# Hybrid encoder layer, attention sweep: GpSimd's half of the softmax sums no longer ordered behind VectorE's, residual additions and four output pieces moved, GpSimd's work placed beside maxima in the short sequence

## The chip, the cores and the metric

One Trainium2 chip, one core of it. The metric is the device time of one execution in microseconds (us). TensorE (PE) does matmuls, its weight loads are PEld; VectorE is DVE, ScalarE is ACT, GpSimd is POOL, SyncE (SP) issues the DMAs. Each engine takes its own instructions strictly in the order in which the program lists them; across engines they wait on semaphores.

## The reference, cut to what matters

One encoder layer runs on two sequences with shared weights: a "prompt" of 1024 tokens (the short one, `s == 0`) and a "sample" of 2048 tokens (`s == 1`), both of width 1024.

```python
h = rms_norm(x, norm_pre)
u_pool, g_pool, q, k, v, g_attn, q_x, g_x = split(h @ w_in)
pool_out = multiscale_pool(u_pool) * silu(g_pool)                     # 256 columns
attn_out = softmax(q k^T / 8) v * silu(g_attn)                        # 8 heads, 2 key heads, 512 columns
x_out    = softmax(q_x k_m^T / 8) v_m * silu(g_x)                     # 4 heads, 256 memory tokens, 256 columns
y = concat(pool_out, attn_out, x_out) @ w_out
return x + rms_norm(y, norm_post)
```

The change is in the softmax sums, the gating, the output product `y` and the last line.

## The kernel before, in words

The first stage (to about 708 us) projects both sequences and puts q, k, v and the gates into DRAM scratch. The second stage is the attention sweep, and the change is all in it. It works through 12 pairs (a pair is 256 query tokens): the sample's eight first (pairs 0 to 7), then the prompt's four (8 to 11). A pair has three groups: key head 0, the memory attention, key head 1 (the first pair has the memory group first). A group with key head 0 or 1 has 16 chunks of 128 keys in the sample and 8 in the prompt; a memory group has 2. A turn does two chunks, so a sample pair takes 17 turns. The order of all instructions on all engines is written out by hand: a loop over turns, and a table `later` of steps that are due at a turn or a fraction of one (`at(turn + 1.1, f, ...)` puts f there, `due` emits it).

In one turn:

- `weights`: PE makes the scores S of a chunk (L231), ACT takes the exponential into P (L233, 128x1024: two heads' halves of 512). P has five buffers.
- `sums`: z, the running sum of the P of a group, is added up elementwise. In the sample `CUT` is 512: DVE adds the upper 512 columns (L244), POOL the lower 512 (L246). In the prompt `CUT` is 0, and DVE adds all 1024 (L244). The odd chunk of a turn is added early in the next turn (`before.sums(kb + 1)`), the even one in the turn itself.
- `largest` looks ahead for a later group: PE scores into the single PSUM buffer N (L189, L181), and DVE takes the maxima of it (L197, L199 after a copy by ACT in L196, or L201). The next N can't start until these have read the last one.
- `values` (L260) multiplies P with V; at a group's end `totals` (L269) has PE sum z over partitions. So totals needs the last L244 and the last L246 of the group.
- `project` adds output pieces (L393 to L395, three matmuls a piece; 8 pieces make one half of an output row block, 32 a pair) in the turns without `values`. When a half is done ACT squares it (L399) and DVE scales it (L411); when both are, POOL makes the norm's factor (L415, L418), ACT scales y (L427), POOL adds the residual into xr (L428), SP stores it (L436).
- `store_mix` is the gating: POOL multiplies a group's result with its gate and 1/z (L304; `pu` is the pooling mixer's tile), ACT casts the high part (L307), POOL subtracts for the low part (L311). Both parts feed the output pieces. In the last pair DVE does this work in POOL's place.

The lines that a sentence can't say:

```python
v = nc.vector.tensor_tensor(out=z[:, cut:], in0=a[:, cut:], in1=P[:, cut:], op=ALU.add)        # L244
e = nc.gpsimd.tensor_tensor(out=z[:, :cut], in0=a[:, :cut], in1=P[:, :cut], op=ALU.add)        # L246
if k < self.chunks - 1:
    behind(e, v)          # POOL's half starts only when DVE's half has ended; not in a group's last chunk
...
HOLD, PIECES = (13, 21), (8, 4)                                                                # L446
for _ in range(PIECES[turns[turn][0].s] if turn < len(turns) else 8):                          # L979
```

Of the kernel before, what the change touches and what calls it, by code (L numbers as in the profile page):

```python
# [23 lines left out]
def encoder(ctx, tc, I, O):  # L24
# [28 lines left out]
    mhalf = const.tile([128, 8], F32, name="mhalf")  # L53
    nc.vector.memset(mhalf, -0.5)

    def behind(later, first):
        tc.add_manual_dep(later.ins, first.ins.name,
                          mybir.DependencyInfo(mybir.DependencyClass.Sync, mybir.DependencyReason.DATA),
                          reason="one after the other")

    def rsqrt(pool, ss, n, count, tag):

# [71 lines left out]
    class Group:  # L134
# [100 lines left out]
        def sums(self, k):  # L235
            if k == 0:
                return
            if k == 1:
                self.z = dbl.tile([128, 2, 512], F32, name="z", tag="z")
            flat = "p j q -> p (j q)"  # L240
            z, P = self.z.rearrange(flat), self.P[k].rearrange(flat)
            a = self.P[0].rearrange(flat) if k == 1 else z
            cut = CUT[self.s]
            v = nc.vector.tensor_tensor(out=z[:, cut:], in0=a[:, cut:], in1=P[:, cut:], op=ALU.add)  # L244
            if cut:
                e = nc.gpsimd.tensor_tensor(out=z[:, :cut], in0=a[:, :cut], in1=P[:, :cut], op=ALU.add)  # L246
                if k < self.chunks - 1:
                    behind(e, v)

        def values(self, ks):  # L250

# [48 lines left out]
    def store_mix(slot, pair, c, a, b, v="p (c t q) -> p c t q"):  # L300

        a, b = a.rearrange(v, c=2, t=2), b.rearrange(v, c=2, t=2)
        e = nc.vector if pair.last else nc.gpsimd
        e.tensor_tensor(out=a, in0=a, in1=b, op=ALU.mult)  # L304

        def high():
            nc.scalar.copy(out=pair.parts()[0][:, c:c + 2], in_=a)  # L307

        def low():
            hi, lo = [m[:, c:c + 2] for m in pair.parts()]  # L310
            e.tensor_tensor(out=lo, in0=a, in1=hi.bitcast(F32), op=ALU.subtract)  # L311

        after = (0, 0, pair.s, pair.s)[c // 2]
        begin = max(slot, pair.free + after)
        soon = pair.s == 0 and not pair.last and c < 4
        at(begin + (0.6 if soon else 1.4), high)
        at(begin + (0.6 if soon else 1.6), low)
# [42 lines left out]
    class Output:  # L360
# [41 lines left out]
        def scale(self, h):  # L402
            if h == 0 and not self.last:
                for m in sorted(later):
                    for x in [x for x in later[m] if x[0].__name__ in ("norm", "out", "store")]:
                        later[m].remove(x)
                        f, args = x
                        f(*((args[0], None) if f.__name__ == "out" else args))
                self.start()
            c = slice(512 * h, 512 * h + 512)  # L410
            nc.vector.tensor_tensor(out=self.y[:, c], in0=self.ps[h], in1=npost[:, c], op=ALU.mult)  # L411
# [8 lines left out]
        def out(self, h, after):  # L420
            x, y = self.xr, self.y
            c = slice(512 * h, 512 * h + 512)
            if self.last:
                nc.vector.scalar_tensor_tensor(out=x[:, c], in0=y[:, c], scalar=self.r[:, 0:1], in1=x[:, c],  # L424
                                               op0=ALU.mult, op1=ALU.add)
            else:
                nc.scalar.activation(out=y[:, c], in_=y[:, c], func=AF.Copy, scale=self.r[:, 0:1])  # L427
                nc.gpsimd.tensor_tensor(out=x[:, c], in0=x[:, c], in1=y[:, c], op=ALU.add)  # L428
            if after is None:
                self.store(h)  # L430
            else:
                at(after, self.store, h)
# [25 lines left out]
    def at(turn, f, *args):  # L458

        later.setdefault(round(turn, 2), []).append((f, args))  # L460
# [8 lines left out]
    fill = []  # L469
# [505 lines left out]
    def project(turn):  # L975

        if turn in value_runs or not fill:
            return
        for _ in range(PIECES[turns[turn][0].s] if turn < len(turns) else 8):  # L979
            out, h, c, start, final = fill.pop(0)  # L980
            out.piece(h, c, start, final, turn >= looked)
            if final:
                out.square(h)
                end = out.last or turn >= len(turns)
                if end:
                    out.scale(h)
                else:
                    at(turn + 1.1, out.scale, h)
                if h == 1:
                    slow = not end and turns[turn][0].s == 1  # L990
                    at(turn + (0.6 if end else 1.6 if slow else 1.4), out.norm)
                    for x in range(2):
                        if out.last:
                            at(turn + 0.6, out.out, x, None)
                        else:
                            z = turn + (2.4 + x if slow else 1.6)
                            at(z, out.out, x, None if end else z + 0.8)
                break

    with tc.manual_schedule(engines=order):  # L1000
        turn = 0
        while turn < len(turns) or later or fill:
# [67 lines left out]
```

## Time and profile before

| what | value |
|---|---|
| time, median of 3 runs | 1760.3 us (1760.29 to 1761.58) |
| the profiled execution: its time, its span | 1756.41 us, 1754.5 us |
| PE busy, share of the span | 1686.4 us, 96% |
| DVE, ACT, POOL busy | 1122.1, 792.3, 830.9 us |
| sample part of the sweep, with the first pair | 708 to about 1440 us |
| prompt part of the sweep | about 1440 to 1754 us |
| L244 (DVE's sums), L246 (POOL's sums), z<-z,P groups | 268.1 us in 272; 299.3 us in 224 |

Busy time is the union of an engine's instructions; idle before a group is the time in which its engine did nothing just before it, and behind the arrow stands what ended that idle time. PEclk is the clock that PE was granted, as a share of full speed.

### The profile page before, as it was taken

How to read it: one execution, taken by the hardware profiler on the slowest of the kernel's cores; microseconds unless marked ns; L12 is line 12 of the kernel's file. 1: busy time of each engine (PE TensorE's matmuls, PEld its weight loads, DVE VectorE, ACT ScalarE, POOL GpSimd, SP SyncE). 2: the span in 40 equal slices, each digit the busy share in tenths (PEclk: the TensorE clock that was granted, in tenths of full speed). 3: DMA queues.
4: the chain of work that ended last, by engine and by line, in shares of the span. 5: the costliest groups of instructions: out<-in, count | busy, mean ns of one | idle time of the engine just before them, and what ended most of it. 6: DMA issues, size and time to landing. Idle time of an engine off the chain costs nothing. (4 is left out here: it accounts for less than half of the span.)

```text
span 1754.5 us, 26096 instructions
## 1 busy us (share of the span) xinstructions
PE 1686.4 (96%) x9400; PEld 1173.4 (67%) x9400; DVE 1122.1 (64%) x1668; ACT 792.3 (45%) x1236; POOL 830.9 (47%) x802
## 2 busy tenths in 40 slices
PE   6899999999999999988999999999999999999998
PEld 6889889798898986434555555555555555556566
DVE  6754316551164425798877878787777858887862
ACT  5532225331252211444565656566565645554541
POOL 4556205570054600488566665667565564341421
PEclk9999999999999999999999999999999999999999
DMA  7543634345443392622121211111121134323222
GB/s 255 174 133 91 180 108 128 120 114 152 122 114 109 108 220 66 170 68 78 49 73 61 67 49 61 68 55 55 49 73 61 55 97 145 103 85 103 67 91 90
DMA packets 151856, 178.32 MB, mean 102 GB/s; under 512 B 20896, under 2 KB 120368, under 8 KB 151728
## 3 DMA queue, kind: packets, MB, share of 16 engines
q1 hardware_dynamic: 151728, 176.65, 34.0%
q8 instruction: 75, 1.23, 0.3%
q14 instruction: 53, 0.43, 0.1%
HBM read 121.26 MB, written 55.20 MB: 101 GB/s over the span
## 5 line engine op out<-in xcount | busy, mean ns | idle before, releaser
L233 ACT ACTIVATE P<-S 128x1024 f32<-128x1024 f32 x344 | 335.2, 1024 | 122.3 <-PE S L231 106.8
L246 POOL TENSOR_TENSOR z<-z,P 128x512 f32<-128x512 f32 x224 | 299.3, 1336 | 161.0 <-DVE z L244 145.2
L260 PE MATMUL acc<-P,V 128*64 128x512 f32 (+1 forms) x1472 | 320.0, 574 | 0.7 <-DVE gate L275 0.2
L244 DVE TENSOR_TENSOR z<-z,P 128x512 f32<-128x512 f32 (+1 forms) x272 | 268.1, 986 | 6.2 <-ACT P L233 5.8
L196 ACT COPY look<-N 128x512 f32<-128x512 f32 x258 | 152.0, 589 | 202.6 <-PE N L189 202.0
L631 PE MATMUL pz<-hT_hi,w_hi 128*128 128x512 f32 x592 | 235.9, 398 | 2.8 <-ACT w_hi L71 1.7
L632 PE MATMUL pz<-hT_lo,w_hi 128*128 128x512 f32 x592 | 233.3, 394 | 0.0
L633 PE MATMUL pz<-hT_hi,w_lo 128*128 128x512 f32 x592 | 231.9, 392 | 0.0
L197 DVE TENSOR_REDUCE nb<-N 128x1 f32<-128x512 f32 x258 | 176.6, 684 | 74.1 <-PE N L189 73.8
L260 PEld LDWEIGHTS acc<-P,V 128*64 128x64 f32 x1472 | 95.8, 137 | 175.6 <-issue 131.3
L231 PE MATMUL S<-q,DH 64*128 64x512 f32 x1280 | 205.5, 399 | 0.0
L199 DVE TENSOR_REDUCE nb<-look 128x1 f32<-128x512 f32 x258 | 175.7, 681 | 43.2 <-ACT look L196 42.3
L66 POOL TENSOR_TENSOR rs<-rs,mhalf 128x4 f32<-128x4 f32 (+2 forms) x76 | 83.8, 1105 | 212.1 <-DVE rs L64 209.2
L189 PE MATMUL N<-KH,q 64*128 64x512 f32 x640 | 148.9, 461 | 8.5 <-DVE nb L201 4.3
L631 PE MATMUL pz<-w_hi,hT_hi 128*128 128x384 f32 (+1 forms) x416 | 141.0, 340 | 2.9 <-ACT hT_hi L71 2.9
L189 PEld LDWEIGHTS N<-KH,q 64*128 64x128 f32 x640 | 61.0, 186 | 120.7 <-issue 73.0
L632 PE MATMUL pz<-w_lo,hT_hi 128*128 128x384 f32 (+1 forms) x416 | 140.1, 337 | 0.8 <-DVE w_lo L72 0.7
L633 PE MATMUL pz<-w_hi,hT_lo 128*128 128x384 f32 (+1 forms) x416 | 139.9, 337 | 0.0
L231 PEld LDWEIGHTS S<-q,DH 64*128 64x128 f32 x1280 | 122.4, 189 | 24.6 <-issue 2.4
L393 PE MATMUL py<-wo_hi,mix 128*128 128x512 f32 x336 | 138.8, 413 | 0.0
L72 DVE TENSOR_TENSOR w_lo<-wraw,w_hi 128x3072 fp32r<-128x3072 f32 (+2 forms) x21 | 67.8, 3228 | 107.7 <-ACT w_hi L71 107.2
L395 PE MATMUL py<-wo_hi,mix 128*128 128x512 f32 x336 | 132.0, 393 | 2.9 <-POOL mix L311 2.9
(155 smaller groups left out, 2752.6 us busy)
## 6 DMA issues: line engine op xcount, KB each, us to landing
wraw<-w_in SPq DMA_DIRECT2D x15, 1536.0 KB
dg<-gst SPq DMA_DIRECT2D x48, 256.0 KB
q<-dq SPq DMA_DIRECT2D x24, 512.0 KB
gz<-rows SPq DMA_DIRECT2D x72, 128.0 KB
x<-x_sample SPq DMA_DIRECT2D x16, 512.0 KB
xr<-x_sample SPq DMA_DIRECT2D x16, 512.0 KB
y_sample<-xr SPq DMA_DIRECT2D x32, 256.0 KB
dq<-qst SPq DMA_DIRECT2D x96, 64.0 KB
```

Of the source, the lines that this page charges most:

```text
L189: nc.tensor.matmul(S[:, 512 * j:512 * j + 512], lhsT=self.q[h, 0, 128 * lane:128 * lane + 128], rhs=KH[self.kind][h, 512 * a:512 * a + 512 ...
L196: c = nc.scalar.copy(out=t[:, 0], in_=S[:, 1])
L197: m = nc.vector.tensor_reduce(out=out[:, 0:1], in_=S[:, 0:1], axis=AX.X, op=ALU.max, negate=True)
L199: nc.vector.tensor_reduce(out=out[:, 1:2], in_=t, axis=AX.X, op=ALU.max, negate=True)
L231: nc.tensor.matmul(S[:, at + x:at + x + w], lhsT=K, rhs=self.q[h, qx, x:x + w], start=False, stop=n == 2, skip_group_check=True)
L233: nc.scalar.activation(out=self.P[k].rearrange("p j q -> p (j q)"), in_=S, func=AF.Exp)
L244: v = nc.vector.tensor_tensor(out=z[:, cut:], in0=a[:, cut:], in1=P[:, cut:], op=ALU.add)
L246: e = nc.gpsimd.tensor_tensor(out=z[:, :cut], in0=a[:, :cut], in1=P[:, :cut], op=ALU.add)
L260: nc.tensor.matmul(self.acc[64 * j:64 * j + 64, x], lhsT=v, rhs=P[:, j, x], start=(k, i) == (0, 0), stop=k == self.chunks - 1, skip_group_ ...
L631: nc.tensor.matmul(ps, lhsT=sh, rhs=mh, start=c == 0, stop=False)
L632: nc.tensor.matmul(ps, lhsT=sh, rhs=ml, start=False, stop=False)
L633: nc.tensor.matmul(ps, lhsT=sl, rhs=mh, start=False, stop=c == n - 1)
```

## The change

- `behind` now takes one instruction and, where a latest DVE sum is noted, makes it wait for that sum. In `sums` the wait of POOL's half on DVE's half is gone. The latest sum is noted only in the prompt (where `cut` is 0), and not in the program's last group; in the sample nothing is noted, so `behind` does nothing there.
- In `store_mix` the POOL instructions (L304, L311) of all pairs but the last, and the residual addition (L428), go through `behind`: in the prompt each waits for the DVE sum emitted last before it.
- `out` now only scales y; the addition is a step `add` of its own, emitted later. In the sample that is 0.8 turn after the scaling, where the next turn's odd chunk has just been summed; the store follows at the next whole turn.
- The pieces in a turn go by the sequence of the output they belong to, not of the turn, until turn `switch` (six turns into the prompt), and are 8 from there on.

```diff
-    def behind(later, first):
-        tc.add_manual_dep(later.ins, first.ins.name, ...
+    latest = []
+    def behind(e):
+        if latest:
+            tc.add_manual_dep(e.ins, latest[-1].ins.name, ...
...
-            v = nc.vector.tensor_tensor(out=z[:, cut:], in0=a[:, cut:], in1=P[:, cut:], op=ALU.add)
+            e = nc.vector.tensor_tensor(out=z[:, cut:], in0=a[:, cut:], in1=P[:, cut:], op=ALU.add)
+            latest[:] = () if cut or turns[-1][0] is self else (e,)
             if cut:
-                e = nc.gpsimd.tensor_tensor(out=z[:, :cut], in0=a[:, :cut], in1=P[:, :cut], op=ALU.add)
-                if k < self.chunks - 1:
-                    behind(e, v)
+                nc.gpsimd.tensor_tensor(out=z[:, :cut], in0=a[:, :cut], in1=P[:, :cut], op=ALU.add)
...
-        e.tensor_tensor(out=a, in0=a, in1=b, op=ALU.mult)
+        m = e.tensor_tensor(out=a, in0=a, in1=b, op=ALU.mult)
+        if not pair.last:
+            behind(m)
...
-            e.tensor_tensor(out=lo, in0=a, in1=hi.bitcast(F32), op=ALU.subtract)
+            m = e.tensor_tensor(out=lo, in0=a, in1=hi.bitcast(F32), op=ALU.subtract)
+            if not pair.last:
+                behind(m)
...
                 nc.scalar.activation(out=y[:, c], in_=y[:, c], func=AF.Copy, scale=self.r[:, 0:1])
-                nc.gpsimd.tensor_tensor(out=x[:, c], in0=x[:, c], in1=y[:, c], op=ALU.add)
+                if after is None:
+                    self.add(h, None)
+                else:
+                    at(after, self.add, h, int(after) + 1)
+                return
+            self.store(h)
+
+        def add(self, h, after):
+            x, y = self.xr, self.y
+            c = slice(512 * h, 512 * h + 512)
+            behind(nc.gpsimd.tensor_tensor(out=x[:, c], in0=x[:, c], in1=y[:, c], op=ALU.add))
             if after is None:
                 self.store(h)
...
-        for _ in range(PIECES[turns[turn][0].s] if turn < len(turns) else 8):
+        for _ in range(PIECES[fill[0][0].s if turn < switch else 0]):
...
-                            at(z, out.out, x, None if end else z + 0.8)
+                            at(z, out.out, x, None if end else z + 0.8 if slow else z + 0.4 + 0.2 * x)
...
+    switch = first[pairs[8].groups[0]] + 6
```

The diff moves lines, so after it L244 is L248, L246 is L251, L304 L307, L311 L316, L411 L418, L428 L445.

The first place is POOL's queue at the end of the key head 0 group of a sample pair (z_8810 is that group's sum, the P numbers rise with the chunk, xr_8806 is the residual of the pair's output under way). Before:

```order
L418 TENSOR_TENSOR rs_9053<-s1_9051,mhalf_123 128x1
L246 TENSOR_TENSOR z_8810<-z_8810,P_9020 128x512
L246 TENSOR_TENSOR z_8810<-z_8810,P_9063 128x512
L428 TENSOR_TENSOR xr_8806<-xr_8806,y_8808 128x512
L311 TENSOR_TENSOR mix_9038<-gate_8259,mix_9037 128x512
L311 TENSOR_TENSOR mix_9038<-gate_8339,mix_9037 128x512
L304 TENSOR_TENSOR pu_9008<-pu_9008,pg_9007 128x512
L246 TENSOR_TENSOR z_8810<-z_8810,P_9071 128x512
L246 TENSOR_TENSOR z_8810<-z_8810,P_9124 128x512
L428 TENSOR_TENSOR xr_8806<-xr_8806,y_8808 128x512
L246 TENSOR_TENSOR z_8810<-z_8810,P_9132 128x512
```

And after:

```order
L425 TENSOR_TENSOR rs_9053<-s1_9051,mhalf_123 128x1
L251 TENSOR_TENSOR z_8810<-z_8810,P_9020 128x512
L251 TENSOR_TENSOR z_8810<-z_8810,P_9063 128x512
L316 TENSOR_TENSOR mix_9038<-gate_8258,mix_9037 128x512
L316 TENSOR_TENSOR mix_9038<-gate_8339,mix_9037 128x512
L307 TENSOR_TENSOR pu_9008<-pu_9008,pg_9007 128x512
L251 TENSOR_TENSOR z_8810<-z_8810,P_9071 128x512
L445 TENSOR_TENSOR xr_8806<-xr_8806,y_8808 128x512
L251 TENSOR_TENSOR z_8810<-z_8810,P_9123 128x512
L251 TENSOR_TENSOR z_8810<-z_8810,P_9131 128x512
L445 TENSOR_TENSOR xr_8806<-xr_8806,y_8808 128x512
```

The second residual addition has moved from before the group's last sum to behind it, and the first from before the three gating instructions to behind them and one more sum. DVE's, ACT's and PE's lists are the same here; on SP the store of the first half moves behind the four small DMAs (L213) of the next group's maxima.

The second place is DVE's queue three turns into the prompt. Before (the last pair of the sample still has output pieces to do; L411 is the scaling of one finished half):

```order
L199 TENSOR_REDUCE nb<-look 128x1
L411 TENSOR_TENSOR y<-py,npost 128x512
L244 TENSOR_TENSOR z<-z,P 128x1024
L197 TENSOR_REDUCE nb<-N 128x1
L199 TENSOR_REDUCE nb<-look 128x1
L208 TENSOR_REDUCE top_5597<-nb 128x8
L129 STREAM_TRANSPOSE rows_13498<-top_5597 128x32
L244 TENSOR_TENSOR z<-z,P 128x1024
L197 TENSOR_REDUCE nb<-N 128x1
L199 TENSOR_REDUCE nb<-look 128x1
L275 TENSOR_TENSOR gate<-acc,gate 128x512
L244 TENSOR_TENSOR z<-z,P 128x1024
```

And after, from the same place:

```order
L203 TENSOR_REDUCE nb<-look 128x1
L248 TENSOR_TENSOR z<-z,P 128x1024
L201 TENSOR_REDUCE nb<-N 128x1
L203 TENSOR_REDUCE nb<-look 128x1
L212 TENSOR_REDUCE top_5597<-nb 128x8
L133 STREAM_TRANSPOSE rows_13483<-top_5597 128x32
L248 TENSOR_TENSOR z<-z,P 128x1024
L201 TENSOR_REDUCE nb<-N 128x1
L203 TENSOR_REDUCE nb<-look 128x1
L278 TENSOR_TENSOR gate<-acc,gate 128x512
L248 TENSOR_TENSOR z<-z,P 128x1024
```

The scaling has left this stretch (it now stands four pairs of maxima later, behind the transpose of the `totals`, L279). On PE four output pieces (12 matmuls, L393 to L395) have left the turn ahead of it, where eight stood in a row, and stand two turns later, directly ahead of the group's `totals`. With ACT's squaring and scaling of that half these are the only rows of PE, ACT and DVE that the change moves.

More of the change, by code (lines that the diff above doesn't have):

```diff
@@ L54, in encoder @@
     nc.vector.memset(mhalf, -0.5)
-    def behind(later, first):
-        tc.add_manual_dep(later.ins, first.ins.name,
-                          mybir.DependencyInfo(mybir.DependencyClass.Sync, mybir.DependencyReason.DATA),
-                          reason="one after the other")
+    latest = []
+    def behind(e):
+        if latest:
+            tc.add_manual_dep(e.ins, latest[-1].ins.name,
+                              mybir.DependencyInfo(mybir.DependencyClass.Sync, mybir.DependencyReason.DATA),
+                              reason="beside a maximum")
     def rsqrt(pool, ss, n, count, tag):
@@ L404, in scale @@
                 for m in sorted(later):
-                    for x in [x for x in later[m] if x[0].__name__ in ("norm", "out", "store")]:
+                    for x in [x for x in later[m] if x[0].__name__ in ("norm", "out", "add", "store")]:
                         later[m].remove(x)
                         f, args = x
-                        f(*((args[0], None) if f.__name__ == "out" else args))
+                        f(*((args[0], None) if f.__name__ in ("out", "add") else args))
                 self.start()
```

## Prediction

> **What bounds the kernel now.** I read the page first, then PE's waits, then the granted clock, then the timelines around the waits. A row of a group or a wait ends in "total us, times, longest" (waits) or "busy us, mean ns | idle before" (groups); a timeline row begins with start and duration.
>
> ```profile
> PE 1686.4 (96%) x9400; PEld 1173.4 (67%) x9400; DVE 1122.1 (64%) x1668; ACT 792.3 (45%) x1236; POOL 830.9 (47%) x802
> ```
>
> PE is the bound; the span is its work plus its holes. PE's waits in the sweep:
>
> ```profile
> PE acc L269 <- POOL z L246: 19.3, 6, 3.6
> ...
> PE py L269 <- POOL z L246: 3.8, 2, 2.2
> ...
> PE N L181 <- DVE top L201: 3.3, 4, 1.0
> ...
> PE py L395 <- POOL mix L311: 2.9, 1, 2.9
> PE N L189 <- DVE nb L197: 2.6, 4, 0.8
> ...
> PE acc L269 <- DVE z L244: 1.7, 1, 1.7
> ```
>
> The largest is one kind of hole: six times the totals wait 3.1 to 3.6 us for GpSimd's last half of a sum. Each such hole has a tail, seen in the granted clock (columns: us, PE busy with its count, clock share, DMA share, GB/s; the sum line covers all six stretches of this kind, of which the first and last are shown):
>
> ```profile
> 937.09:940.50 3.41, 3.41 (x20) 0.50 0.64 223
> ...
> 1425.19:1428.61 3.42, 3.42 (x18) 0.50 1.02 298
> sum 23.90, PE 23.22; mean PE 3.87
> ```
>
> After every one of the six PE runs at half clock, for 23.2 busy us together, which costs half of that, 11.6 us. Short holes have no such tail: behind the 1.7 us wait on L244 the clock stays whole, behind the 2.2 us one in the first pair it drops.
>
> ```profile
> 797.14:800.55 3.41, 3.41 (x18) 0.50 0.23 93
> ...
> 1498.00:1501.40 3.40, 3.35 (x30) 1.00 0.97 286
> ```
>
> So six holes are worth 19.3 + 11.6 = 30.9 us, and a hole that is left counts only with its own length once it is under about 1.7 us. The Trainium skill ("TensorE: Matmul & The Clock Gate", section "HAM oscillation — how this bites in real kernels") gives as its rule no PE-idle gaps over about 3.4 us. By that rule only the sixth hole, of 3.6 us, could lower the clock and five half-clock stretches would have another cause and stay, some 9.7 us less gain; the trace disagrees, a hole of 2.2 us is followed by a half clock here.
>
> **Part 1, the sample's sums and the moved addition.** Why is GpSimd late? One of the six ends, GpSimd's rows, then ACT's exponentials and a cast, then PE's arrival:
>
> ```profile
> 1013.30 1.28 POOL L246 TENSOR_TENSOR z<-z,P 128x512 f32<-128x512 f32 x1 [0.72 <-DVE z L244]
> 1014.54 1.29 POOL L311 TENSOR_TENSOR mix<-pu,mix 128x512 fp32r<-128x512 f32 x1
> 1015.79 1.75 POOL L311 TENSOR_TENSOR mix<-gate,mix 128x512 fp32r<-128x512 f32 x1
> 1017.64 0.86 POOL L415 TENSOR_SCALAR s<-ssy 128x1 f32<-128x1 f32 x1
> 1018.59 0.56 POOL L418 TENSOR_TENSOR rs<-s,mhalf 128x1 f32<-128x1 f32 x1
> 1019.11 2.65 POOL L246 TENSOR_TENSOR z<-z,P 128x512 f32<-128x512 f32 x2
> 1021.72 1.73 POOL L428 TENSOR_TENSOR xr<-xr,y 128x512 f32<-128x512 f32 x1
> 1023.41 2.96 POOL L311 TENSOR_TENSOR mix<-gate,mix 128x512 fp32r<-128x512 f32 x2
> 1026.34 1.28 POOL L304 TENSOR_TENSOR pu<-pu,pg 128x512 f32<-128x512 f32 x1
> 1027.59 3.09 POOL L246 TENSOR_TENSOR z<-z,P 128x512 f32<-128x512 f32 x2
> 1030.64 1.26 POOL L428 TENSOR_TENSOR xr<-xr,y 128x512 f32<-128x512 f32 x1
> 1031.86 1.26 POOL L246 TENSOR_TENSOR z<-z,P 128x512 f32<-128x512 f32 x1
> ```
>
> ```profile
> 1009.11 1.94 ACT L233 ACTIVATE P<-S 128x1024 f32<-128x1024 f32 x2
> ...
> 1011.91 0.65 ACT L307 CAST mix<-gate 128x512 fp32r<-128x512 f32 x1
> 1014.71 1.94 ACT L233 ACTIVATE P<-S 128x1024 f32<-128x1024 f32 x2 [2.15 <-PE S L231]
> ...
> 1020.28 1.94 ACT L233 ACTIVATE P<-S 128x1024 f32<-128x1024 f32 x2
> ```
>
> ```profile
> 1033.17 1.08 PE L269 MATMUL acc<-z,ones 128*32 128x256 f32 x8 [3.13 <-POOL z L246]
> ```
>
> GpSimd works without a hole from 1013.30 to the end of the last sum at 1033.1; PE is there at 1030.0 (3.13 before 1033.17). The last six sums use the three pairs of exponentials shown. The first of them could start when its exponential ends, at 1010.1 (the pair from 1009.11, about 0.97 each), but stands behind DVE's half until 1013.30. New order, each operation at its plain 1.28 us and no meeting with DVE: sum 1010.1 to 1011.4; the two low parts wait for ACT's casts, of which the second ends at 1012.56, so about 1012.0 to 1014.6; norm 0.86 + 0.56 and its gaps, 1.6, to 1016.2; two sums (data there since 1015.7) to 1018.8; two low parts to 1021.3; pooling gate to 1022.6; sum to 1023.9; first addition to 1025.2; two sums to 1027.7. The second addition comes behind. Of the 5.4 us gained, 1.3 is that addition's place, the rest is the earlier start and the absence of meetings.
>
> Meetings are not absent, however:
>
> ```profile
> 1017.68 0.65 DVE L244 TENSOR_TENSOR z<-z,P 128x512 f32<-128x512 f32 x1
> ...
> 1021.01 1.30 DVE L244 TENSOR_TENSOR z<-z,P 128x512 f32<-128x512 f32 x1
> ```
>
> An addition of DVE alone takes 0.65, under a running GpSimd addition 1.30, and GpSimd's own row goes from 1.28 to 1.73: one waits while the other works. So each of DVE's five additions between 1012 and 1027 can push GpSimd back by up to 0.65: 0 to 3.3 us, and the last sum ends between 1027.7 and 1031.0, the middle 1029.4 against PE at 1030.0. The hole left is 0 to 1.0 us; I take 0.3. All are under 1.7, so no half clock. Gain of the six: 19.3 - 1.8 + 11.6 = 29.1 us.
>
> The cost is DVE's. One pair's stretch (97 us of a period of 97.6): the engines' busy time is in the order PE, PEld, DVE, ACT, POOL.
>
> ```profile
> 1035.00:1132.00 97.00, 93.86 (x558) 54.07 (x560) 74.66 (x117) 57.17 (x82) 58.61 (x47) 0.98 0.19 60
> ```
>
> ```profile
> L244 DVE TENSOR_TENSOR z<-z,P 128x512 f32<-128x512 f32 x28 | 23.5, 838 | 0.0
> L197 DVE TENSOR_REDUCE nb<-N 128x1 f32<-128x512 f32 x32 | 22.0, 686 | 9.3 <-PE N L189 9.3
> L199 DVE TENSOR_REDUCE nb<-look 128x1 f32<-128x512 f32 x32 | 21.9, 683 | 6.5 <-ACT look L196 6.5
> ```
>
> GpSimd's two sums now follow the two exponentials at once, 2.6 us of every turn's 5.6 (1009.11 to 1014.71 to 1020.28), and DVE's two additions lie about half a turn apart, so about every second one meets GpSimd. If none more meets, the cost is 0. If all 31 additions (the row's 28 and the 3 that open a group) take 1.30 in place of 0.84, DVE gets 14.3 us more. Halfway is 7 us. DVE stands idle 9.3 + 6.5 = 15.8 us in front of maxima, waiting for PE and ACT, and takes the delay out of that: the maxima come no later on average, and its work of 75 + 7 = 82 us, at most 89, stays under PE's 92.5 (97.6 less 3.2 less 1.9). Where one turn has more DVE work PE will wait for a maximum now and then: between 0 and 0.15 us a turn (a quarter of one 0.65 lengthening), 0 to 18 us over seven pairs of 17 turns; I take 0.03, 3.5 us, nearer the lower end because of the 15.8. On SP the store of a first half leaves the place ahead of the next maxima's DMAs, and the second addition ends at about 1030.7 in place of 1031.9, so the residual's buffer comes free no later.
>
> **Part 2, the first pair, 708 to 826 us.** Here DVE, not PE, sets the pace, and its additions already meet GpSimd:
>
> ```profile
> L244 DVE TENSOR_TENSOR z<-z,P 128x512 f32<-128x512 f32 x39 | 42.8, 1098 | 0.0
> ```
>
> At 1.30 they cost 39 x 0.2 = 7.9 us more. Against that stand the two waits on L246 of 3.8 us, the half clock of 1.7 (797.14 above) and the wait on L311 of 2.9, 8.4 together, all for a GpSimd that is late. Bounds -8 to +8; I take 0.
>
> **Part 3, four and four.** Twelve matmuls leave the turn ahead of the first prompt group's last sums and stand directly before its totals, and DVE loses one scaling (L411) ahead of them. These are the twelve in their old place (columns as for the clock; the thirteenth is the end of the one before):
>
> ```profile
> 1484.11:1486.88 2.77, 2.77 (x13) 1.00 0.13 13
> ```
>
> That stretch has two of the waits above: 0.8 (longest on L197) and 1.7 (on L244). DVE's sums there:
>
> ```profile
> 1489.57 1.52 DVE L244 TENSOR_TENSOR z<-z,P 128x1024 f32<-128x1024 f32 x1
> ...
> 1492.66 2.30 DVE L244 TENSOR_TENSOR z<-z,P 128x1024 f32<-128x1024 f32 x1
> ```
>
> DVE had idled before, so it starts 2.8 us sooner and is done when PE has run the moved pieces. Both waits go: 0 to 2.5 (no loss, since PE's work is the same and DVE has less ahead of it), I take 2.5.
>
> **Part 4, GpSimd beside maxima in the prompt.** Those 1.52 and 2.30 are met by a gate and a residual addition; alone such a sum takes about 1.2. Another one before a wait of PE:
>
> ```profile
> 1536.20 1.94 DVE L244 TENSOR_TENSOR z<-z,P 128x1024 f32<-128x1024 f32 x1
> ```
>
> With GpSimd's operation behind the sum it runs beside the two maxima (0.69 + 0.68 of one turn, GpSimd's 1.28) and the sum is 0.7 shorter. Three of the four waits on L201 (1.0 each) follow such a sum and lose 0.7: 2.1 us; of the rest of the waits on L197, 1.8, I take a quarter. The waiting operation holds up only GpSimd's next ones, and those who wait for them (ACT's cast, then the pieces) have a turn or more. Bounds -2 (one late low part, as the 2.9 above) to +4; I take 2.5.
>
> **Sum.** 29.1 - 3.5 + 0 + 2.5 + 2.5 = 30.6 us. The profiled execution took 1756.4, so 1725.8; the median of the runs is 3.9 higher, and against it I predict 1760.3 - 30.6, about 1730 us.
>
> **The rivals.**
> - DVE becomes late at maxima. One lengthening of 0.65 reaches PE in every third turn: 17/3 x 0.65 = 3.7 us a pair, 26 over seven, in place of the 3.5: 1752, at best 1745 with fewer. For it: PE's single N buffer. Against: 15.8 us of idle time per pair.
> - GpSimd stays late. Meetings use up what the start gains; a hole of 1.8 us with its half clock stays six times: 6 x 1.4 = 8.4 gained in place of 29.1, so 1750. For it: 1.73 and 1.75 rows already now; against: even the upper bound above leaves 1.0.
> - Slower: the meeting is a full block each time. Without its 31 additions of 0.84 DVE has 74.7 - 26.0 = 48.7 us of work a pair; at 1.41 us an addition it fills PE's 92.5, and it decides from 1.58, where it fills the present 97.6. At 1.65 it is 99.9, 2.3 more than now, seven times, less 5 of parts 3 and 4: 1771. For it: the 2.30 row of part 3, 1.2 us of work that waited out most of a GpSimd operation. Against: only about every second one meets GpSimd at all. The Trainium skill ("SBUF — State Buffer", section "SBUF: two separate sides") says that such a pair shares a port as an exclusive lock, the loser blocked for the whole instruction; the 1.30 and 1.73 rows agree, and this rival is what it would do if every addition lost.
> - The half clock has another cause and stays: 9.7 less, 1740.
> - Nothing: GpSimd's halves were never held up by more than they catch up, and the six holes stay: about 1758.
>
> **How the numbers follow.** My forecast 0.66, with its own range 1721 to 1740 (parts 2 and 4 at their ends); DVE late 0.12; GpSimd late 0.09; clock 0.03; nothing 0.05; slower 0.05. The range 1720 to 1751 takes in the first four. A measurement of this kernel can tell about 0.2%, 3.5 us, from no change: faster 0.66 + 0.12 + 0.09 + 0.03 = 0.90, within 0.05, slower 0.05.
>
> **What would show it.** Right: no wait "PE acc L269 <- POOL z" over 1 us; the clock at 1.00 through the sample from 840 us; pair period near 93 us; L244 in 512 columns up from 0.84 to about 1.0 to 1.1, POOL's idle time before L246 on DVE gone; no 1.7 wait at the boundary; prompt sums near 1.2. Wrong: PE's waits on L197 in the sample grow beyond 5 us, DVE busy over 95% of a pair, or holes over 1.7 us remain at the totals.

## The result, and the profile after

The changed kernel takes 1715.1 us in the median of four runs (1713.7 to 1717.0), against 1760.3 before: a ratio of 0.9751, with a 95% interval of 0.9725 to 0.9778. The forecast was 1730 with a range from 1720, so the direction was right and the gain lies outside the range: 45 us where 30 were forecast. The profiled execution took 1714.31 us (span 1712.5), 42.1 less than that of before. In the four later batches the kernel before took 1758.1 to 1758.9 us in the median of 9 to 23 executions, so some 1.4 to 2.2 of the 45 us may lie in the few executions of the first comparison. The changed kernel was not run again in those batches: a difference of about 2 us from its 1715.1 can't be told from none.

The first row of the page, PE's waits from 700 us to the end (total us, times, longest), and one row over the sweep from 826 to 1640 us, the sample and most of the prompt (us, then busy us of PE, PEld, DVE, ACT and POOL with their counts, clock share, DMA share, GB/s):

```profile
PE 1674.6 (98%) x9400; PEld 1167.3 (68%) x9400; DVE 1141.4 (67%) x1668; ACT 791.0 (46%) x1236; POOL 852.9 (50%) x802
```

```profile
PE N L193 <- DVE nb L205: 5.1, 9, 1.3
PE N L185 <- DVE top L205: 1.2, 4, 0.3
PE N L193 <- DVE nb L201: 1.0, 2, 0.5
PE N L193 <- ACT gst L864: 0.7, 1, 0.7
PE N L193 <- ACT P L237: 0.4, 1, 0.4
PE acc L272 <- POOL z L251: 0.4, 1, 0.4
PE N L185 <- DVE nb L205: 0.3, 1, 0.3
```

```profile
826.00:1640.00 814.00, 810.79 (x4961) 475.54 (x4958) 676.70 (x1002) 480.31 (x694) 473.40 (x358) 1.00 0.24 76
```

Of the six holes at the totals one of 0.4 us is left, no wait on the gating is left, and the clock is whole. Where a group of key head 0 ends (the place of the forecast's replay), GpSimd now reads so (start, duration):

```profile
1013.77 1.30 POOL L445 TENSOR_TENSOR xr<-xr,y 128x512 f32<-128x512 f32 x1
1015.03 2.99 POOL L251 TENSOR_TENSOR z<-z,P 128x512 f32<-128x512 f32 x2
1017.98 1.28 POOL L445 TENSOR_TENSOR xr<-xr,y 128x512 f32<-128x512 f32 x1
```

The last sum ends at 1018.02, and PE starts the totals at 1018.19: 0.17 us to spare, and about as much (0.17 to 0.20) in five of the six places; in the sixth PE waits the 0.4. GpSimd is on time by little.

The two traces can be compared stage by stage, from the first totals to the last (PE's starts of totals, before against after):

| stage | forecast | measured in the traces | what it was before |
|---|---|---|---|
| first stage, to the first totals | - | -1.3 | the same instructions in both; a difference of two executions |
| first pair and the start of the second (716.7 to 840.1 us; after 718.0 to 833.2) | 0 | 8.2 | waits of 12.2 us (now 6.1), one half clock of 1.7 |
| sample's pairs 1 to 7 (to 1472.5; 1436.0) | 29.1 - 3.5 | 29.7 | six holes of 19.3 us, six half clocks |
| boundary (to 1497.9; 1458.8) | 2.5 | 2.6 | waits of 0.8 and 1.7 us |
| prompt (to 1714.4; 1672.3) | 2.5 | 2.9 | waits on maxima |
| sum | 30.6 | 42.1 | |

### The profile page after: what moved, and what is told of

Same layout as the page of the kernel before. It is cut to its first block, busy times and chain, and to the rows that moved or that the text cites. A ratio compares the mean times of both kernels' runs of the same rounds, so it can differ in the third digit from the quotient of the medians.

```text
span 1712.5 us, 26086 instructions
## 1 busy us (share of the span) xinstructions
PE 1674.6 (98%) x9400; PEld 1167.3 (68%) x9400; DVE 1141.4 (67%) x1668; ACT 791.0 (46%) x1236; POOL 852.9 (50%) x802
## 5 line engine op out<-in xcount | busy, mean ns | idle before, releaser
L251 POOL TENSOR_TENSOR z<-z,P 128x512 f32<-128x512 f32 x224 | 334.9, 1495 | 144.0 <-ACT P L237 136.7
L248 DVE TENSOR_TENSOR z<-z,P 128x512 f32<-128x512 f32 (+1 forms) x272 | 286.4, 1053 | 5.7 <-ACT P L237 5.5
L201 DVE TENSOR_REDUCE nb<-N 128x1 f32<-128x512 f32 x258 | 176.5, 684 | 48.1 <-PE N L193 47.5
L235 PE MATMUL S<-q,DH 64*128 64x512 f32 x1280 | 201.2, 392 | 0.0
L400 PE MATMUL py<-wo_hi,mix 128*128 128x512 f32 x336 | 139.0, 414 | 0.0
L401 PE MATMUL py<-wo_lo,mix 128*128 128x512 f32 x336 | 131.6, 392 | 0.0
```

The costliest lines, as they stand in the source:

```text
L201: m = nc.vector.tensor_reduce(out=out[:, 0:1], in_=S[:, 0:1], axis=AX.X, op=ALU.max, negate=True)
L235: nc.tensor.matmul(S[:, at + x:at + x + w], lhsT=K, rhs=self.q[h, qx, x:x + w], start=False, stop=n == 2, skip_group_check=True)
L248: e = nc.vector.tensor_tensor(out=z[:, cut:], in0=a[:, cut:], in1=P[:, cut:], op=ALU.add)
L400: nc.tensor.matmul(ps, lhsT=mh, rhs=wo_hi[:, c, cols], start=first, stop=False)
```

## The experiments

The first theory: the first pair's term was mis-sized, and the order between the halves alone gives about 8 us there (theory A). Its rivals: the first pair's gain came with something else (B), or the addition's place carries the sample's six holes (C). Four kernels do one part of the change alone, from the kernel before.

### Only the order between halves removed

```diff
-                if k < self.chunks - 1:
-                    behind(e, v)
```

> The kernel before with only the order between the two halves of a sum taken out; the residual addition stays where it was. Two theories on why the gain was larger than forecast. Theory A (the first pair's term was mis-sized): the order alone gives the first pair about 8 us (its late-GpSimd waits and half clock go, and DVE pays nothing for it) and shortens the six holes at the sample's totals to about 1.1 us each, since the addition still stands ahead of the last sum (1.28 us) and the changed kernel had 0.16 us to spare there; no half clock stays. Gain 19.3 - 6.6 + 11.6 + 8 = 32 us, a time of about 1728. Theory B (the first pair gains nothing from the order; what the changed kernel saved there came with something else): 24 us, about 1736. Theory C (the addition's place carries the six holes, the order little): holes over 2 us with their half clock stay, gain under 16 us, 1744 or more.

Measured: 1729.75 us (5 runs), ratio to before 0.9835 (0.9822 to 0.9848). Its waits on GpSimd in the whole sweep are one row:

```profile
PE acc L267 <- POOL z L246: 7.4, 6, 1.6
```

Theory A to 2 us: the first pair's waits on GpSimd are gone, and the six holes have shrunk to about 1.16 us five times and 1.61 once. From the first totals to those of the second pair's first group this trace takes 115.3 us, the changed kernel's 115.2 and before's 123.4: the order alone gives all of the first pair's 8.2. So the order is two thirds of the gain, and B and C fall. One thing differs from theory A, by which no half clock stays: behind the two waits at the boundary, 0.77 and 1.73 us close together, PE runs at half clock for 6.8 us here, some 3 us more, where before's clock stayed whole behind the same two waits.

```profile
1468.30:1475.12 6.82, 6.15 (x32) 3.75 (x34) 5.20 (x8) 2.50 (x3) 0.00 (x0) 0.50 0.65 194
```

### Only the addition moved

```diff
+                if apart:
+                    at(after, self.add, h, int(after) + 1)
+                    return
                 nc.gpsimd.tensor_tensor(out=x[:, c], in0=x[:, c], in1=y[:, c], op=ALU.add)
...
-                            at(z, out.out, x, None if end else z + 0.8)
+                            at(z, out.out, x, None if end else z + 0.8, slow)
```

> The kernel before with only the residual addition moved to a step of its own, 0.8 turn later, in the sample's turns; the order between halves stays. Theories A and B: each of the six holes gets shorter by the addition's 1.28 us, from 3.13 to about 1.85. If a half clock follows every hole over about 1.7 us, all six stay and the gain is 6 x 1.3 = 8 us (1752); if a hole of 1.85 no longer lowers the clock, it is 8 + 11.6 = 19 us (1741). Theory C: the holes close almost wholly, gain 25 us or more (1735 or less). The first pair has no such addition and must keep its waits on the late GpSimd (3.8 us on totals, 2.9 on the gating) in all three.

Measured: 1749.84 us, ratio 0.9951 (0.9938 to 0.9964), 9 us faster. The waits, and the 3.41 us behind the first and the third of the six holes (1.91 and 1.94 us long):

```profile
PE acc L269 <- POOL z L246: 12.1, 6, 2.4
PE py L269 <- POOL z L246: 3.8, 2, 2.2
PE py L395 <- POOL mix L311: 2.9, 1, 2.9
```

```profile
939.27:942.68 3.41, 3.41 (x18) 2.79 (x18) 3.02 (x5) 1.47 (x2) 1.79 (x2) 0.50 0.20 77
1130.85:1134.26 3.41, 3.41 (x32) 2.21 (x34) 2.74 (x5) 1.95 (x3) 2.37 (x2) 1.00 0.29 105
```

Each hole is shorter by the addition's 1.2 us, as expected, and the first pair keeps its waits. But the half clock follows a hole of 1.9 us four times and stays away twice, once behind one of 1.9 and once behind one of 2.4: length alone doesn't decide it ("What a hole costs"). The trace of before showed that already, though the forecast did not use it: behind the 2.9 us wait on the gating, which ends at 826.10, its clock was whole (columns here: PE busy, clock share, DMA share, GB/s).

```profile
826.10:829.50 3.40, 3.36 (x16) 1.00 0.27 78
```

### Only the pieces, and only the prompt's part

```diff
-        for _ in range(PIECES[turns[turn][0].s] if turn < len(turns) else 8):
+        for _ in range(PIECES[fill[0][0].s if turn < switch else 0]):
```

> The kernel before with only the new rule for the number of output pieces in a turn. The forecast's own term: the waits of 0.8 and 1.7 us at the boundary between sample and prompt go, 2.5 us (time about 1758, 0.14% less); the rest of the trace stays as before. Rival: the twelve matmuls that now stand directly ahead of the totals only move the wait to another place, 0 us.

> The kernel before with only the prompt's part: GpSimd's gating and additions wait for the last DVE sum, and the additions of the prompt's turns stand on a step of their own; the sample's order between halves, its additions and the pieces stay as before. The forecast's own term: prompt sums of 1024 columns fall from 1366 ns in the mean to near 1200 and the waits on maxima fall by 2.5 us (time about 1758). In the changed kernel the prompt's waits on maxima were 2.2 us in place of 5.1, so 2.9 us. Rival: the waits fell there because of the pieces, and alone this part gives under 1 us.

The second kernel is the changed one with the sample's order, its additions and the old rule for pieces put back. Measured: 1755.41 us for the pieces (0.9974, 0.9963 to 0.9986) and 1754.54 for the prompt (0.9982, 0.9973 to 0.9991). Both are 3.5 and 4.4 us under the median of before, 1 to 1.5 us more than their terms. The pieces take both waits at the boundary away; one of 0.8 us, which before did not have, stands later in the prompt. The prompt's part leaves these waits from 1440 us on:

```profile
PE acc L275 <- DVE z L248: 2.1, 1, 2.1
PE N L185 <- DVE top L205: 1.2, 4, 0.3
PE N L193 <- DVE nb L201: 1.1, 2, 0.5
```

The maxima's waits are 2.3 us, as in the changed kernel (2.2), so they fell by this part and not by the pieces; the wait at the boundary (2.1) stays without the pieces. DVE's prompt sums, before and in the changed kernel, from 1440 to 1700 us (mean ns behind the busy us):

```profile
L244 DVE TENSOR_TENSOR z<-z,P 128x1024 f32<-128x1024 f32 x43 | 58.7, 1366 | 1.5 <-ACT P L233 1.5
```

```profile
L248 DVE TENSOR_TENSOR z<-z,P 128x1024 f32<-128x1024 f32 x48 | 61.1, 1273 | 1.7 <-ACT P L237 1.5
```

### The first pair: which order makes it late

In the changed kernel the order was kept in the first pair alone (`first_ordered`):

```diff
             if cut:
-                nc.gpsimd.tensor_tensor(out=z[:, :cut], in0=a[:, :cut], in1=P[:, :cut], op=ALU.add)
+                m = nc.gpsimd.tensor_tensor(out=z[:, :cut], in0=a[:, :cut], in1=P[:, :cut], op=ALU.add)
+                latest[:] = (e,) if self.early and k < self.chunks - 1 else ()
+                behind(m)
```

> The changed kernel with the order between halves kept in the first pair alone (its three groups, up to about 826 us); everything after it as changed. Theory A: the first pair's waits of totals and gating on GpSimd (6.7 us before) and its half clock (1.7) come back, 8 us slower than the changed kernel (1723 against 1715), and DVE's additions in the first pair stay at about 1.1 us in either case. Theory B: the first pair's gain had another cause, the time is that of the changed kernel within 2 us, and the waits do not come back.

Its median was about 1721 us, without a profile of the sweep that could be read; so it was run again, beside the kernel before with the order removed in the first pair alone (`and not self.early` added to the old condition):

> The same kernel as the one before with the order kept in the first pair alone: of that run there is no profile of the sweep to read, and its times lay about 6 us above the changed kernel. Theory A (the order alone makes GpSimd late in the first pair): the waits of totals and gating on GpSimd come back with 1.6, 2.2 and 2.9 us, with a half clock or two, and DVE's additions there stay at about 1.1 us; 1721 to 1723. Theory B: the profile shows other waits, or none, in the first pair.

> The kernel before with the order between halves taken out in the first pair alone. Theory A: the counterpart of the kernel above, 8 us faster than before (about 1751), no wait on GpSimd in the first pair, the six holes of 3.1 to 3.6 us and their half clocks unchanged; of DVE's 43 additions in the first pair as many overlap a GpSimd operation as before (37), so that DVE pays nothing. Theory B and the forecast's own term: within 2 us of the kernel before.

Measured: 1721.08 us (0.9787, 0.9773 to 0.9800) and 1752.8 in the median of four executions (0.9966, 0.9952 to 0.9980). The waits on GpSimd in the first kernel, then in the second:

```profile
PE py L274 <- POOL z L250: 3.8, 2, 2.2
PE acc L274 <- POOL z L250: 0.4, 1, 0.4
```

```profile
PE acc L269 <- POOL z L246: 19.3, 6, 3.6
PE py L395 <- POOL mix L311: 2.9, 1, 2.9
```

The medians differ from the changed kernel's by 6.0 us and from before's by 5.7, not by the 8 of theory A, so B falls, but theory A was only half right. With the order in the first pair the two waits at its totals come back, and with them 4.4 us of the stage's 8.2, but the 2.9 us wait on the gating doesn't; without it in the first pair alone, that wait stays. So it has another cause, the order in the second pair, whose first sums start at about 795 us, ahead of the first pair's output pieces. The test is the same edit with `(self.s, self.p) == (1, 1)`:

> The changed kernel with the order between halves kept in the second pair alone (its groups run from about 826 us on). Theory A': the hole of 2.9 us ahead of the first output pieces (for GpSimd's low part of the pooling mixer, which stands in GpSimd's queue behind the second pair's first sums) and a half clock come back, 3 to 4.5 us slower than the changed kernel (1718 to 1720), the first pair's waits stay away, and no hole comes back at the totals of the second pair, which had none before. Rival (that wait came from the first pair's own late sums): the hole does not come back, within 1 us of the changed kernel.

Measured: 1717.41 us (0.9770, 0.9756 to 0.9784), 2.3 above the changed kernel; that is less than the 3 to 4.5 expected, and the executions of the two overlap, so the trace decides. The wait, the clock behind it, and GpSimd from 795 us in this kernel:

```profile
PE py L404 <- POOL mix L318: 2.9, 1, 2.9
```

```profile
821.26:824.68 3.42, 3.42 (x10) 2.42 (x8) 0.03 (x1) 0.00 (x0) 3.34 (x3) 0.50 0.28 78
```

```profile
795.25 1.28 POOL L250 TENSOR_TENSOR z<-P 128x512 f32<-128x512 f32 x1 [3.39 <-DVE z L248]
797.23 1.30 POOL L250 TENSOR_TENSOR z<-z,P 128x512 f32<-128x512 f32 x1 [0.69 <-DVE rz L289]
798.49 1.28 POOL L125 TENSOR_TENSOR wo_lo<-raw,wo_hi 128x512 fp32r<-128x512 f32 x1
800.46 1.27 POOL L250 TENSOR_TENSOR z<-z,P 128x512 f32<-128x512 f32 x1 [0.69 <-DVE z L248]
802.43 1.29 POOL L250 TENSOR_TENSOR z<-z,P 128x512 f32<-128x512 f32 x1 [0.70 <-DVE z L248]
...
819.48 1.26 POOL L318 TENSOR_TENSOR mix<-pu,mix 128x512 fp32r<-128x512 f32 x1
```

The hole and its half clock are back, and the stage from the first totals to those of the second pair's first group is 3.8 us longer than in the changed kernel; with the 4.4 above that makes the 8.2. GpSimd stands idle 5.5 us in front of four sums, waiting for DVE, and is busy without a break from 802 us to the low part that PE needs, at 819.48; in the changed kernel the idle time there is 2.2 us. Both places in which the first pair was late are shown.

### What a hole costs

The changed kernel, with an in-place multiplication by one on GpSimd ahead of the last sum of key head 0's group, longer from pair to pair:

```diff
+    DOSE = (0, 240, 440, 600, 760, 920, 1080, 1320)
...
+                n = DOSE[self.p] if self.kind == 0 and k == self.chunks - 1 else 0
+                for i in range(-(-n // 512)):
+                    x = z[:, :min(512, n - 512 * i)]
+                    nc.gpsimd.tensor_scalar(out=x, in0=x, scalar1=1.0, scalar2=None, op0=ALU.mult)
```

> The changed kernel with extra work on GpSimd ahead of the last sum of key head 0's group in the sample's pairs 1 to 7: a multiplication by one, in place, over 240, 440, 600, 760, 920, 1080 and 1320 columns, an amount that rises from pair to pair. It makes holes of PE of rising length at the same totals as before, some 0.5 to 3.2 us if a column costs what it does in the sums (1.28 us for 512). The forecast's price: a hole costs its own length and, from about 1.7 us on, 1.7 us more (3.41 us at half clock). Expected: no half clock behind holes under 1.7 us, one behind each over 2.2 us, 0.9 to 1.0 of the clock elsewhere; together about 12.6 + 3 to 4 x 1.7 = 18 to 20 us slower than the changed kernel. Rival (a half clock comes only behind holes over 3.4 us): 12 to 13 us slower and no half clock. Rival (a half clock behind every hole over 0.5 us): 24 us slower.

Measured: 1737.69 us, 22.6 slower than the changed kernel and more than the 18 to 20 expected: the holes came out at 16.8 us together, not 12.6. Pairs 1 and 2 have holes of 0.43 and 1.19 us; those of pairs 3 to 6 are these, and behind them the clock of 3.41 us each:

```profile
1024.22 0.64 PE L276 MATMUL acc<-z,ones 128*32 128x256 f32 x8 [1.88 <-POOL z L255]
1118.98 1.08 PE L276 MATMUL acc<-z,ones 128*32 128x256 f32 x8 [2.31 <-POOL z L255]
1215.57 0.64 PE L276 MATMUL acc<-z,ones 128*32 128x256 f32 x8 [2.71 <-POOL z L255]
1312.39 0.64 PE L276 MATMUL acc<-z,ones 128*32 128x256 f32 x8 [3.67 <-POOL z L255]
```

```profile
1024.22:1027.63 3.41, 3.41 (x32) 2.21 (x34) 2.69 (x5) 1.90 (x3) 2.42 (x2) 1.00 0.19 77
1118.63:1122.05 3.42, 3.07 (x18) 1.87 (x20) 1.66 (x3) 0.58 (x1) 2.76 (x3) 0.50 0.20 77
1215.57:1218.98 3.41, 3.41 (x32) 2.18 (x34) 2.69 (x5) 1.90 (x3) 2.43 (x2) 1.00 0.20 77
1313.19:1316.60 3.41, 3.41 (x18) 2.66 (x18) 2.93 (x5) 1.61 (x2) 1.62 (x2) 0.50 0.20 77
```

The hole of 2.31 us is followed by a half clock, that of 2.71 is not. The half clocks start at 1118.63 and 1313.19, 57 times 3.413 apart: on a fixed grid. (So do before's: its seven half-clock stretches, from 797.14 to 1425.19, start 41, 28, 29, 29, 28 and 29 such steps apart.) An edge of that grid lies at 1214.20 (28 steps behind 1118.63), in the middle of the 2.71 us hole, which so has 1.34 us on one side and 1.37 on the other; the 2.31 us hole has 1.96 in one window, that of 3.67 has 2.61. All seven holes (the last, of 4.63, halves the clock for two windows) agree with: the clock halves for a window when about half of the one before it was idle. The traces put the edge between 1.6 and 1.8 us of idle time in a window, without a sharp value: 1.67 halved it once in the kernel with the moved addition, 1.80 did not there. A window that is itself at half clock takes less to be followed by another one. Before's second hole, 3.13 us long, had 2.62 in one window and 0.51 in the next, and the clock was half for two windows (columns: PE busy, clock share, DMA share, GB/s):

```profile
1032.66:1039.49 6.83, 6.32 (x32) 0.50 0.43 154
```

The 0.35 us that the 2.31 us hole leaves in its half-clock window did not do that. The rival "a half clock behind every hole over 0.5 us" falls with the 1.19, 1.88 and 2.71 us holes. The rival "over 3.4 us only" falls with the 2.31 us hole; it is also the rule of the Trainium skill that the forecast weighed ("TensorE: Matmul & The Clock Gate", section "HAM oscillation — how this bites in real kernels"), which this run disagrees with.

### What DVE's added work costs

The changed kernel with one more maximum a turn on DVE, over more columns from pair to pair:

```diff
+    DOSE = (0, 0, 128, 256, 384, 512, 768, 1024)
...
                 g.sums(k)
+                if g.s == 1 and DOSE[g.p]:
+                    nc.vector.tensor_reduce(out=spare, in_=npost[:, :DOSE[g.p]], axis=AX.X, op=ALU.max)
```

> The changed kernel with one more maximum on DVE in each of the sample's turns from the third pair on (over 128, 256, 384, 512, 768 and 1024 columns in pairs 2 to 7; 0.68 us for 512 alone), which nothing waits for. It asks how near DVE was to holding PE up, the term that the forecast sized at 3.5 us. DVE is busy 79 of 92.4 us a pair now, so a mean of 0.79 us more a turn would fill it. Theory A (DVE's idle time in front of maxima takes a delay up until it is nearly used up): no wait over 0.3 us a turn in pairs 2 to 4 (up to 0.5 us more), the first clear waits at 0.68, and at 1.0 and 1.3 us DVE is the bound, about 4 and 9 us longer a pair; in all 12 to 18 us slower than the changed kernel. Rival (single delays already reach PE, as the forecast had it): every pair from the second dose on longer by a fifth or more of its dose, 1 us at 0.36 a turn, 2 at 0.5, 4 at 0.68, in all over 22 us slower.

Measured: 1735.68 us, 20.6 slower than the changed kernel, between the 18 of theory A and the 22 of its rival. But the output product's matmuls were slower too, 395 ns in the median in place of 389, even in the prompt, which has no added maximum; the one thing changed there is the place of the tiles. Three kernels take this apart: the result in a tile of 64 bytes, the result in an existing tile, and the tile of 64 bytes without the added maxima.

> The kernel with one more maximum a turn again, with its result in a tile of 64 bytes in place of 4. In the first form the output product's matmuls (the three of a piece) took 395 ns each in the median in place of 389, in the prompt too, where no maximum was added; tiles allocated behind the result lay 4 bytes further on. If that shift is the cause, they take 389 again and the kernel is about 6 us faster than the first form (1730 in place of 1735.7); what is left of its loss, some 14 us against the changed kernel, is then the price of DVE's work, a fifth of the 69 us added. If the added work slows them, 395 stays.

> The kernel with added maxima a third time (128, 256, 384, 512, 768 and 1024 columns in pairs 2 to 7), with the result in an existing tile, so that no tile moves. If the shift of tiles had made the matmuls slower: 389 ns again and a loss of about 14 us (1729), a fifth of the 69 us added, which is then the price of DVE's work alone; a fifth in every pair says that part of a single delay reaches PE though DVE has idle time, as the forecast had it; nothing in the first three doses and most of it in the last two says that the idle time takes it up. If the added work slows the matmuls: 395 and 1736 as before.

> The changed kernel with one more tile of 64 bytes a partition allocated where the kernels with added maxima had theirs, set once and used by nothing. If the place of the tiles behind it in SBUF makes the output product's matmuls slower, they take 395 ns in the median in place of 389 and the kernel is about 6 us slower than the changed one (1721); if not, 389 and 1715, and the 395 came with the added maxima.

Measured: 1737.54, 1734.57 and 1719.90 us. The matmuls took 394 to 398 ns (medians of the three lines), 389 and 394 to 398: the added maxima are not their cause, an unused 64 bytes are. One of the three matmuls of a piece from 1440 to 1690 us, in the changed kernel, then with the unused tile:

```profile
L401 PE MATMUL py<-wo_lo,mix 128*128 128x512 f32 x120 | 46.9, 390 | 0.0
```

```profile
L401 PE MATMUL py<-wo_lo,mix 128*128 128x512 f32 x120 | 47.5, 395 | 0.0
```

With no tile moved, each of the six pairs, from the key head 1 totals of the pair before it to its own, against the changed kernel's. Here are the first and the last but one, first with the added maxima, then without (columns as in the row from 826 us):

```profile
882.28:975.56 93.28, 93.15 (x565) 53.45 (x564) 82.64 (x135) 57.18 (x82) 63.51 (x47) 1.00 0.19 63
...
1259.94:1357.30 97.36, 94.48 (x565) 53.55 (x564) 93.30 (x136) 57.18 (x82) 64.81 (x47) 1.00 0.18 58
```

```profile
881.89:974.41 92.52, 92.52 (x566) 53.36 (x565) 78.74 (x118) 57.15 (x82) 63.35 (x47) 1.00 0.19 64
...
1252.50:1344.89 92.39, 92.39 (x565) 53.30 (x564) 78.74 (x118) 57.16 (x82) 63.56 (x47) 1.00 0.19 62
```

The six pairs are longer by 0.8, 1.8, 2.2, 2.4, 5.0 and 6.4 us for 4.7, 6.9, 9.2, 11.5, 16.0 and 20.5 us of added work (17 maxima of 0.27 to 1.21 us): a sixth to a third of it reaches PE, from the smallest dose on, long before DVE is full. That is the rival's side, though the whole loss, 19.5 us, is above the 14 expected.

### Two attempts at the first pair's remaining waits

```diff
-            cut = CUT[self.s]
+            cut = 576 if self.early else CUT[self.s]
```

> The changed kernel with the halves cut at 576 in place of 512 columns in the first pair alone: GpSimd takes 64 columns more of each sum, DVE 64 less. There PE still waits 6.1 us for DVE's maxima. If DVE's own work sets the pace there, its 40 additions get 0.08 us shorter each, 3.2 us, and the waits fall by about 2 us; if GpSimd comes late again (40 x 0.16 = 6.4 us more work in a stretch in which it is busy 99 of 118 us), the waits of totals on it come back and it is slower by 2 to 8 us. Likeliest within 3 us of the changed kernel either way.

```diff
-            g.largest(n, turn >= 23)
+            g.largest(n, turn >= 1)
```

> The changed kernel with the scores of the first pair's look-ahead read as in the later ones: ACT copies one half (0.6 us), DVE takes the maximum of the other half (0.68) and then of the copy, in place of one maximum over both halves (1.23). It is an attempt at the 6.1 us for which PE still waits there. If those waits are for the reading of the one buffer N, it comes free 0.55 us earlier each time, and 3 to 4 us of the eleven waits go (1711 to 1712). If DVE's total work sets the pace (45 more instructions, 0.13 us more for each pair of maxima, 6 us on an engine that is busy 106 of 118 us), the waits stay or grow: 0 to 4 us slower.

Measured: 1716.70 us (0.9764, 0.9744 to 0.9785), no difference that can be told from the changed kernel's; and 1722.60 (0.9798, 0.9784 to 0.9811), 7 us slower, beyond the 4 that were expected at most. In the second kernel PE waits 10.3 us for DVE's first maxima in the first pair, where the changed kernel's largest such row is 5.1, and 4.3 us for ACT:

```profile
PE N L193 <- DVE nb L201: 10.3, 15, 1.3
```

Reading N sooner does not help there. That DVE's total work sets the pace fits (it is busy 109.2 of 118 us in place of 106.0), but the waits on ACT's copies came with it, and the two were not separated. Neither beats the changed kernel.

## Why the prediction was wrong, and where it was right

**The step that failed is Part 2, the first pair: 0 forecast, 8.2 measured.** It set 7.9 us of longer DVE additions against 8.4 us of late-GpSimd waits and half clock. The 8.4 came back nearly whole. The 7.9 did not exist; DVE's additions of the first pair, 708 to 826 us, became no longer (1098 ns before):

```profile
L248 DVE TENSOR_TENSOR z<-z,P 128x512 f32<-128x512 f32 x40 | 42.6, 1065 | 0.0
```

Counted in the traces by overlap (over 0.1 us), 37 of 43 additions there met a GpSimd operation before, 39 of 44 after, and 38 of 43 in the kernel with the order taken out of the first pair alone. The order had kept a sum's two halves apart, but not GpSimd's half from DVE's next additions: nothing was left to lose. The forecast had written that the additions "already meet GpSimd" and then still charged them the full 1.30 us. And the wait on the gating, which it booked with the first pair, belongs to the second pair's order.

**The price of DVE's lengthening, Part 1's 3.5 us, was not paid.** DVE's part of a pair now (1018.2 to 1110.6 us):

```profile
L248 DVE TENSOR_TENSOR z<-z,P 128x512 f32<-128x512 f32 x28 | 27.5, 984 | 0.0
L201 DVE TENSOR_REDUCE nb<-N 128x1 f32<-128x512 f32 x32 | 21.9, 685 | 4.7 <-PE N L193 4.7
L203 DVE TENSOR_REDUCE nb<-look 128x1 f32<-128x512 f32 x32 | 21.8, 682 | 6.1 <-ACT look L200 6.1
```

The additions went from 838 to 984 ns, 4.0 us a pair and not the 7 of the middle value; of those from 840 to 1420 us 134 of 196 meet GpSimd by over 0.1 us, 91 of 186 before. The idle time in front of maxima fell from 15.8 to 10.8 us, and PE does not wait for DVE in the sample's pairs 1 to 7 (the waits listed above lie in the first pair, at the boundary and in the prompt). GpSimd carries as much: its sums between 840 and 1380 us went from 1318 to 1487 ns.

```profile
L246 POOL TENSOR_TENSOR z<-z,P 128x512 f32<-128x512 f32 x154 | 203.0, 1318 | 125.7 <-DVE z L244 117.0 <-DVE rz L284 7.9
```

```profile
L251 POOL TENSOR_TENSOR z<-z,P 128x512 f32<-128x512 f32 x165 | 245.4, 1487 | 128.7 <-ACT P L237 123.6
```

Added maxima cost PE a sixth of their time at the smallest dose. By that rate 4.0 us would have cost 0.7 a pair, about 5 in seven, so 3.5 was no unlikely price; but the sample's stage leaves at most 0.4 us for it (30.1 gained at the holes, 29.7 measured). Why the longer additions come free where added maxima do not was not separated.

**What held.** Part 1's main term: the six holes and their clocks were priced at 30.9, forecast at 29.1, and gave 30.1 (19.3 less the 0.4 left and a wait of 0.4 on ACT, and 11.6); the sample with its DVE term is 4.1 above the forecast. The bounds of the replay, 2.3 us ahead of PE to 1.0 behind it, hold the measured 0.17 us ahead. The tail: without the holes there is no half clock in the sweep. Part 3 (2.6 for 2.5) and Part 4 (2.9 for 2.5); in Part 4 three of the four waits on the maxima of L201 fell from 1.03 to 0.31 us, the 0.7 forecast, though the sums fell only to 1273 ns and not near 1200. The pair period of 92.4 is the forecast 93.

**What the numbers missed beside that.** The traces' 42.1 less the 30.6 is 11.5: 8.2 for the first pair, 4.1 for the sample, 0.5 for parts 3 and 4, less 1.3 for the first stage, in which nothing changed. The other 3 us to 1715.1 come from the anchor, and are chance: the profiled execution of before lay 3.9 under the median, that of after 0.8. The range reached down only to the forecast's own terms at their good ends; the first pair's "-8" alone would have put 1722, and no case had it together with a DVE that pays nothing.

## What to carry to other kernels

Before charging a meeting of two engines for a change, count how many operations meet already: a meeting can be lost only once. An order between two halves also delays everything queued behind the later half, in another stage than the one where the wait shows, so look for late consumers well past the order's own group. And price holes by the window they fall in, not by their length alone.

## What was not expected of the hardware

- The half clock goes by a fixed grid of 3.41 us and by the idle time within one window: holes of 1.9 us halved the clock four times, holes of 2.4 and 2.71 us, cut by an edge, did not, and one of 3.13 us halved it for two windows. So a hole of about 2 to 3 us costs nothing more, 1.7 or about 3 us more, by where it lies on the grid, and the grid lies differently in each execution.
- 64 unused bytes a partition, allocated ahead of later tiles, made each of the output product's matmuls 5 ns slower (395 in place of 390) and the kernel 4.8 us slower (1719.9 against 1715.1). Which address matters was not tried.
